# A decoder layer in split fp32 on one core: LN1's high parts written from PSUM, first weights cast behind h, Silu's table loaded early

## The chip, the cores and the metric

The kernel runs on one core of a Trainium2 chip. The metric is the device time of one execution in microseconds. A core has TensorE (PE, with PEld its weight loads), VectorE (DVE), ScalarE (ACT), GpSimd (POOL) and SyncE (SP), which issues most of the DMAs. Every engine works through its own list of instructions in order and waits on semaphores for the others.

## What is computed

One layer of a decoder with 512 prompt positions and 8 decode rows, model width 1024, all in fp32:

```python
h = x * (1 + scale) + shift                      # adaLN, from silu(c) @ w_ada + b_ada
aq, ak, av, mq, mk, mv, mo, mi, mf = split(h @ w_in)
att = block_sparse_attention(aq, ak, av)         # decode rows read a paged K/V cache
mem = mlstm(mq, mk, mv, mi, mf)                  # 4 heads of 128, matrix memory C, state n, m
mix = concat(att, norm(mem) * g * sigmoid(mo)) @ w_out
x = layernorm(ALPHA * x + (1 + g1) * mix)        # LN1
h = x * (1 + sc2) + sh2                          # called h2 below
f = (silu(h @ w_gate) * (h @ w_up)) @ w_down     # FFN, inner width 2816
y = layernorm(ALPHA * x + (1 + g2) * f)
```

Returned are y, the new K/V rows and the new mLSTM states, for prompt and decode rows.

## The kernel before

**Products.** An fp32 product is made of three passes (`three`, L400): each operand is split into a high part, rounded to the matmul type fp32r, and a low part, the rest, and high x high, high x low and low x high are added in PSUM. The high part is a cast on ScalarE, the low part a subtraction on VectorE. For weights this is `prepare_one` (cast whi at L232, subtraction wlo at L233, tiles of 128x1024), for activations `split_hidden` (L403: cast at L404, subtraction at L405).

**Order.** The program's order is made when it is built. Pieces of work are generators ("lanes"); each `tick` lets every lane that is due run to its next `yield n`, which puts it off by n ticks, then prepares one weight tile and issues the weight loads for which a buffer is free, all on SP's queue in one fixed stream. Between the ticks TensorE's large products are written. So the number behind `yield` decides behind which pieces of the products a lane's next instructions stand, on every engine.

**First phase** (`first_phase`). The first input projection runs over five chunks of the 1024 input columns while adaLN's first two vectors are still being made. For chunk i: `first_ada` (product with w_ada, copy of ada_sb on ScalarE, transposes ps_adat on TensorE), the split of the chunk's weights (`first_split`: whi, wlo of wq at L534 and L535, the same for wk_s at L537), then `first_h`: adaT, two operations of VectorE from ps_adat (L494); h on VectorE and, at the same time, its high part straight from x on ScalarE (L511); its low part; the decode rows' h (hsT) and its small cast hT_hi at the end (L520, L404). `first_main` are the products of six column blocks; those with 0 to 3 use whi and wlo.

**Decode rows of the mLSTM** (`sample_mlstm`). It ends with h8, which four small transposes (L1543, ps_h) bring into the layout of the output product's operand. Around them on TensorE stand the passes of the output product's first half, and the last prompt states: products ps_C (L1197) that ScalarE copies to Csb (L1200), and the sums ps_n (L1168), whose four rows are copied by ScalarE and VectorE in turn (L1172). When the decode rows are there, `ln_rows` may load the rows lg and lb of LN1's affine part, which ScalarE multiplies later (L1620).

**LN1** (`ln1_tile`, one per tile of 128 positions). The output product has two halves (`out_product`): tiles 0 and 1, then tiles 2 and 3. When both column halves of a tile are out of PSUM and added to x (`residual`, L1631 and L1632), `ln1_tile` makes the statistics and normalises x, and some ticks later, for each half of 512 columns: four transposes into one PSUM bank (L1699, ps_h), four operations of ScalarE with scale a2 and bias b2 that write v in SBUF (L1703), the two casts h_hi (L404) and the two subtractions h_lo (L405). These are h2's parts for the FFN.

**FFN.** `ffn_first` begins while tiles 2 and 3 are in LN1; its Silu (L1813) loads ScalarE's table for that function when it comes to it. From there on TensorE runs through the FFN's weights.

Of the kernel before, what the change touches and what calls it, by code (L numbers as in the profile page):

```python
# [13 lines left out]
AF = mybir.ActivationFunctionType  # L14
ALU = mybir.AluOpType
AX = mybir.AxisListType.X

P = 128
# [28 lines left out]
def decoder_layer(  # L47
# [61 lines left out]
    TT = nc.vector.tensor_tensor  # L109
    TS = nc.vector.tensor_scalar  # L110
# [3 lines left out]
    ACT = nc.scalar.activation  # L114
# [288 lines left out]
    def split_hidden(dst_hi, dst_lo, v):  # L403
        ACOPY(out=dst_hi, in_=v)  # L404
        TT(out=dst_lo, in0=v, in1=dst_hi, op=ALU.subtract)  # L405
# [151 lines left out]
    def first_phase():  # L557
        n = len(chunks)
        for i in range(n):
            sb = first_ada(i)  # L560
            if i:
                first_split(i)
            if i + 3 < n:
                load_first(i + 3)
                if i + 4 == n:
                    later_loads()
            elif i + 2 >= n:
                pump_loads()
            if i:
                first_main(i - 1, (3,))  # L570
            first_h(i, sb)
            if i:
                first_main(i - 1, (4, 5))
            if i + 1 == n:
                prepare_one()
                prepare_one()
            first_main(i, (0, 1, 2))
        first_main(n - 1, (3, 4, 5))
# [817 lines left out]
    junk = cst.tile([P, P], F32, name="junk")  # L1396
# [99 lines left out]
    def sample_mlstm(lag):  # L1496
# [16 lines left out]
        ps = yield from lane_bank("ps_nu")  # L1513
# [23 lines left out]
                bias=s[:, 13, h:h + 1])  # L1537
        yield 1
        TT(out=h8, in0=h8, in1=o_s, op=ALU.mult)
        yield 2  # L1540
        ps = yield from lane_bank("ps_h8")
        for h in range(HM):
            nc.tensor.transpose(ps[:, ts(h, 8)], h8[:, ts(h, P)], ident[:NB, :NB])  # L1543
# [35 lines left out]
    a2 = cst.tile([P, KD, 9], F32, name="a2")  # L1579
# [107 lines left out]
    def ln1_tile(t):  # L1687
        s = ln1_stats[t]
        nc.vector.bn_stats(out=s[:, 6:12], in_=x1[t][:, 512:D])
        nc.vector.bn_aggr(out=s[:, 12:14], in_=s[:, 0:12])  # L1690
        rsqrt(s[:, 14:15], s[:, 13:14])
        TS(out=x1[t], in0=x1[t], scalar1=s[:, 12:13], scalar2=s[:, 14:15], op0=ALU.subtract, op1=ALU.mult)
        yield 9 if t < 2 else 5
        while not h2_hi:
            yield 1
        for half in range(2):
            ps = yield from lane_bank("ps_h2")
            for kk in range(4):
                nc.tensor.transpose(ps[:, ts(kk, P)], x1[t][:, ts(4 * half + kk, P)], ident)  # L1699
            v = yield from slot(rows, "v2", spare=1)  # L1700
            for kk in range(4):
                k = 4 * half + kk
                ACT(out=v[:, ts(kk, P)], in_=ps[:, ts(kk, P)], func=AF.Identity,  # L1703
                    scale=a2[:, k, 8:9], bias=b2[:, k, 8:9])
            banks.put(ps)
            v3 = v[:, 0:512].rearrange("p (k q) -> p k q", q=P)
            for i in range(2):
                split_hidden(h2_hi[2 * half + i][:, :, ts(t, P)], h2_lo[2 * half + i][:, :, ts(t, P)],
                             v3[:, 2 * i:2 * i + 2, :])
            rows.put(v)  # L1710
        h2_done[0] += 1
        while not ffn.get(("f", 1)):
            yield 1
        yield 2 * t
        for n in range(2):
            PT_(out=x1[t][:, ts(n, 512)], in0=x1[t][:, ts(n, 512)], in1=big2["lg"][n], op=ALU.mult)
            PT_(out=x1[t][:, ts(n, 512)], in0=x1[t][:, ts(n, 512)], in1=big2["lb"][n], op=ALU.add)
        x1_done[0] += 1
# [393 lines left out]
    nc.gpsimd.memset(ffn["fsT"], 0.0)  # L2112
    ffn["sacc"] = get("sacc", [512])
    state["spill"] = 2
    ffn_first(2)
    state["spill"] = 0

# [81 lines left out]
```

## Time and profile before

| | us |
|---|---|
| median of 3 runs | 788.52 (786.09 to 791.42) |
| the profiled execution's own time | 786.77 |
| its span in the profile | 785.1 |
| mean granted clock of TensorE | 0.993 of full |
| TensorE busy | 752.9 (96%) |
| VectorE busy | 405.3 (52%) |
| ScalarE busy | 276.5 (35%) |

All rows come from the one profiled execution, and their times count from the start of its span. What lies between span and execution time is 1.7 us.

A row of a timeline gives the start, the duration, engine, line, operation, result<-operands and how many instructions are drawn together; the brackets at the end give the time that the engine stood idle before it and what ended that. Line numbers are those of the kernel before; in the changed kernel they are one or two smaller or some larger, as the diff moves them.

### The profile page before, as it was taken

What the parts mean: (1) busy time and instruction counts of PE and PEld (TensorE: products, weight loads), DVE (VectorE), ACT (ScalarE), POOL (GpSimd) and SP (SyncE); (2) the same over time, 40 slices, a digit from 0 to 9 for tenths busy, and PEclk for the clock granted to TensorE, in tenths of its full rate; (3) what the DMA queues carried; (4) which work ended last, traced back from release to release, by engine and by line L of the source; (5) the groups of instructions that cost most, each with busy time, mean ns of one, the idle gap of its engine ahead of it and who ended that gap; (6) DMA issues with size and microseconds to landing.
All of it is one profiled execution on the core that took longest, in us unless ns stands there. A gap on an engine that the chain in (4) does not pass through costs nothing.

```text
span 785.1 us, 14709 instructions
## 1 busy us (share of the span) xinstructions
PE 752.9 (96%) x5798; PEld 620.7 (79%) x5798; DVE 405.3 (52%) x850; ACT 276.5 (35%) x560; POOL 140.3 (18%) x163
## 2 busy tenths in 40 slices
PE   8899999899989998899899999999999999999995
PEld 6678667688755667656799977999987799999675
DVE  3442378977345487588653434333332342332687
ACT  2341466545343346536442211223221122322300
POOL 2010235342000122000029413100001130000011
PEclk9999999999999999999999999999999999999998
DMA  8965885664678968746523425323223323223002
GB/s 334 375 221 146 264 266 176 213 215 136 196 244 282 292 236 172 274 152 192 148 59 105 136 84 154 87 84 106 91 74 89 97 81 108 82 81 108 1 30 81
DMA packets 105906, 123.11 MB, mean 157 GB/s; under 512 B 8220, under 2 KB 65696, under 8 KB 105836
## 3 DMA queue, kind: packets, MB, share of 16 engines
q1 hardware_dynamic: 97796, 112.97, 45.9%
q10 hardware_dynamic: 7976, 9.20, 3.4%
q8 instruction: 45, 0.74, 0.4%
q14 instruction: 25, 0.20, 0.1%
q0 software_dynamic: 64, 0.01, 0.0%
HBM read 114.98 MB, written 7.17 MB: 156 GB/s over the span
## 4 chain that ended last, share of the span: by engine, by line
PE 70%; DVE 10%; DMA 4%; ACT 4%; issue 3%; SPq 1%; POOL 1%; ACTq 0%; POOLq 0%; DVEq 0%
PE acc L657 35%; PE acc L398 21%; DVE wlo L233 2%; PE ps_dn L420 1%; PE ps_ada L412 1%; PE accl L398 1%; DVE rtmp L1631 1%; PE ps_sc L815 1%; ACT whi L232 1%; DVE x L1632 1%; PE ps_pt L848 1%; PE ps_o L878 1%; DMA raw<-in_w_ada_dram 1%; PE ps_num L1084 1%; DMA s_scr<-s_sb 1%
## 5 line engine op out<-in xcount | busy, mean ns | idle before, releaser
L233 DVE TENSOR_TENSOR wlo<-raw,whi 128x1024 fp32r<-128x1024 f32 x104 | 137.0, 1324 | 120.8 <-ACT whi L232 114.0
L232 ACT CAST whi<-raw 128x1024 fp32r<-128x1024 f32 x104 | 107.9, 1049 | 156.4 <-issue 65.7
L657 PE MATMUL acc<-h_lo,whi 128*128 128x256 f32 (+1 forms) x640 | 129.0, 283 | 0.0
L657 PE MATMUL acc<-h_hi,wlo 128*128 128x256 f32 (+1 forms) x640 | 129.0, 283 | 0.0
L657 PE MATMUL acc<-h_hi,whi 128*128 128x256 f32 (+1 forms) x640 | 128.7, 282 | 0.0
L657 PEld LDWEIGHTS acc<-h_hi,whi 128*128 128x128 f32 x640 | 99.1, 188 | 2.7 <-issue 2.5
L657 PEld LDWEIGHTS acc<-h_hi,wlo 128*128 128x128 f32 x640 | 99.5, 188 | 0.0
L657 PEld LDWEIGHTS acc<-h_lo,whi 128*128 128x128 f32 x640 | 98.6, 188 | 0.0
L1236 POOL TENSOR_TENSOR kpage<-kpage,qb 128x512 f32<-128x512 f32 x32 | 43.3, 1374 | 74.9 <-DMA kpage<-in_cache_k_dram 72.0
L1780 DVE TENSOR_TENSOR vf<-acc,vf 128x256 f32<-128x256 f32 x20 | 8.5, 425 | 73.6 <-PE acc L657 73.6
L398 PE MATMUL acc<-whi,f_hi 128*128 128x512 f32 x112 | 45.3, 405 | 0.0
L398 PE MATMUL acc<-wlo,f_hi 128*128 128x512 f32 x112 | 44.3, 395 | 0.0
L398 PE MATMUL acc<-whi,f_lo 128*128 128x512 f32 x112 | 44.2, 394 | 0.0
L398 PE MATMUL acc<-whi,hT_hi 128*128 128x512 f32 x96 | 43.1, 449 | 0.0
L1786 POOL COPY fsT<-vf 128x8 f32<-128x8 f32 x20 | 4.8, 240 | 193.4 <-DVE vf L1781 193.4
L404 ACT CAST f_hi<-vf 128x512 fp32r<-128x512 f32 (+1 forms) x24 | 14.0, 585 | 68.0 <-DVE vf L1781 62.0
L398 PE MATMUL acc<-whi,hT_lo 128*128 128x512 f32 x96 | 38.0, 396 | 0.0
L398 PE MATMUL acc<-wlo,hT_hi 128*128 128x512 f32 x96 | 37.8, 394 | 0.0
L1632 POOL TENSOR_TENSOR x<-x,rtmp 128x512 f32<-128x512 f32 x16 | 26.0, 1646 | 65.1 <-DVE rtmp L1631 64.7
L657 PE MATMUL acc<-hT_hi,whi 128*128 128x256 f32 (+1 forms) x160 | 35.7, 304 | 0.0
L657 PE MATMUL acc<-hT_lo,whi 128*128 128x256 f32 (+1 forms) x160 | 32.3, 283 | 0.0
L657 PE MATMUL acc<-hT_hi,wlo 128*128 128x256 f32 (+1 forms) x160 | 32.3, 283 | 0.0
(403 smaller groups left out, 1407.0 us busy)
## 6 DMA issues: line engine op xcount, KB each, us to landing
raw<-in_w_ada_dram SPq DMA_DIRECT2D x32, 512.0 KB
raw<-in_w_in_dram SPq DMA_DIRECT2D x22, 512.0 KB
raw<-in_w_gate_dram SPq DMA_DIRECT2D x44, 256.0 KB
raw<-in_w_up_dram SPq DMA_DIRECT2D x44, 256.0 KB
raw<-in_w_down_dram SPq DMA_DIRECT2D x22, 512.0 KB
raw_a<-in_ada_first_dram SPq DMA_DIRECT2D x16, 512.0 KB
kpage<-in_cache_k_dram SPq DMA_DIRECT2D x32, 256.0 KB
vpage<-in_cache_v_dram SPq DMA_DIRECT2D x32, 256.0 KB
```

The source lines that it names most:

```text
L232: ACOPY(out=t.hi_t, in_=t.raw)
L233: TT(out=t.lo_t, in0=t.raw, in1=t.hi_t, op=ALU.subtract)
L398: mm(ps, lhsT=a, rhs=b, start=start and i == 0, stop=stop and i == n - 1)
L404: ACOPY(out=dst_hi, in_=v)
L412: mm(ps[32 * c:32 * c + 32, 0:P], lhsT=lhs[:, k0 + kk, :], rhs=raw3[:, kk, ts(c, P)], start=start and kk == 0, stop=stop and kk == nk - 1, ...
L420: mm(ps[32 * c:32 * c + 32, 0:256], lhsT=lhs[:, k0 + kk, :], rhs=raw3[:, kk, ts(n, 256)], start=start, stop=stop, tile_position=(0, 32 * c))
L657: mm(accs[d, hf][:, 0:hi - lo], lhsT=w, rhs=two(xx, k)[:, lo:hi], start=k == 0 and i == 0, stop=k == 7 and i == 2)
L815: mm(bs[e][:, 0:n], lhsT=two(qT, pair)[eh, ts(qt, P)], rhs=two(kT, pair)[eh, 0:n], start=True, stop=True, tile_position=(64 * e, 0))
L848: nc.tensor.transpose(ps[:, ts(kt, P)], pr[:, ts(kt, P)], ident)
L1236: PT_(out=ks[i - 4], in0=ks[i - 4], in1=qb, op=ALU.mult)
L1632: (PT_ if pool_add else TT)(out=dst, in0=dst, in1=tmp, op=ALU.add)
L1780: TT(out=v[:, 0:HALF], in0=a[:, 0:HALF], in1=v[:, 0:HALF], op=ALU.mult)
```

## The change

Four edits. (1) In the first phase, from the second chunk on, `first_split` comes after `first_h`. (2) In `sample_mlstm` the lane waits four ticks, not two, ahead of its transposes. (3) In `ln1_tile` ScalarE writes the high part directly from PSUM, in four operations; VectorE computes v from the same PSUM bank, and the low part is v less the high part. The two casts from v are gone. (4) Ahead of the FFN's first products ScalarE runs a Silu on one element of a scratch tile.

```diff
--- before.py
+++ after.py
@@ -558,8 +558,6 @@
         n = len(chunks)
         for i in range(n):
             sb = first_ada(i)
-            if i:
-                first_split(i)
             if i + 3 < n:
                 load_first(i + 3)
                 if i + 4 == n:
@@ -570,6 +568,7 @@
                 first_main(i - 1, (3,))
             first_h(i, sb)
             if i:
+                first_split(i)
                 first_main(i - 1, (4, 5))
             if i + 1 == n:
                 prepare_one()
@@ -1537,7 +1536,7 @@
                 bias=s[:, 13, h:h + 1])
         yield 1
         TT(out=h8, in0=h8, in1=o_s, op=ALU.mult)
-        yield 2
+        yield 4
         ps = yield from lane_bank("ps_h8")
         for h in range(HM):
             nc.tensor.transpose(ps[:, ts(h, 8)], h8[:, ts(h, P)], ident[:NB, :NB])
@@ -1700,13 +1699,15 @@
             v = yield from slot(rows, "v2", spare=1)
             for kk in range(4):
                 k = 4 * half + kk
-                ACT(out=v[:, ts(kk, P)], in_=ps[:, ts(kk, P)], func=AF.Identity,
+                ACT(out=h2_hi[k // 2][:, k % 2, ts(t, P)], in_=ps[:, ts(kk, P)], func=AF.Identity,
                     scale=a2[:, k, 8:9], bias=b2[:, k, 8:9])
+                TS(out=v[:, ts(kk, P)], in0=ps[:, ts(kk, P)], scalar1=a2[:, k, 8:9], scalar2=b2[:, k, 8:9],
+                   op0=ALU.mult, op1=ALU.add)
             banks.put(ps)
             v3 = v[:, 0:512].rearrange("p (k q) -> p k q", q=P)
             for i in range(2):
-                split_hidden(h2_hi[2 * half + i][:, :, ts(t, P)], h2_lo[2 * half + i][:, :, ts(t, P)],
-                             v3[:, 2 * i:2 * i + 2, :])
+                hi, lo = h2_hi[2 * half + i][:, :, ts(t, P)], h2_lo[2 * half + i][:, :, ts(t, P)]
+                TT(out=lo, in0=v3[:, 2 * i:2 * i + 2, :], in1=hi, op=ALU.subtract)
             rows.put(v)
         h2_done[0] += 1
         while not ffn.get(("f", 1)):
@@ -2112,6 +2113,8 @@
     nc.gpsimd.memset(ffn["fsT"], 0.0)
     ffn["sacc"] = get("sacc", [512])
     state["spill"] = 2
+
+    ACT(out=junk[0:1, 0:1], in_=junk[0:1, 0:1], func=AF.Silu)
     ffn_first(2)
     state["spill"] = 0
```

Since lanes set the order, edit (2) moves more than it touches. The places on which the steps stand follow; a row is an engine's instruction (source line, operation, result<-operands, size, what it waits for), in the order of the list, and "x3" stands for three like rows.

ScalarE in the first phase, third chunk, before: ada_sb is the copy of the chunk's adaLN product, whi and wk_s are its weights, the two ACTIVATEs are the high part of h.

```order
L470 COPY ada_sb<-ps_ada 128x128 [waits PE_49]
L534 CAST whi<-wq 128x1024 [waits DMAHW0_49]
L537 CAST wk_s<-wk_90 128x512 [waits DMAHW1_49,Activation_49]
L511 ACTIVATE hT_hi<-xT,adaT 128x512 [waits DMAHW7_49,DVE_49]
L511 ACTIVATE hT_hi<-xT,adaT 128x512
L404 CAST hT_hi<-hsT 128x2x8 [waits DVE_49]
```

ScalarE there, with the change:

```order
L470 COPY ada_sb<-ps_ada 128x128 [waits PE_49]
L511 ACTIVATE hT_hi<-xT,adaT 128x512 [waits DMAHW7_49,DVE_49,Activation_49]
L511 ACTIVATE hT_hi<-xT,adaT 128x512
L404 CAST hT_hi<-hsT 128x2x8 [waits DVE_49]
L534 CAST whi<-wq 128x1024 [waits DMAHW0_49]
L537 CAST wk_s<-wk_90 128x512 [waits DMAHW4_49,DMAHW1_49]
```

The weights' casts have moved behind the decode rows' cast from hsT, which waits for VectorE. VectorE's wlo and the low part of wk_s have moved likewise, behind hsT.

TensorE before, around the decode rows' transposes (ps_h_4335; `acc` are passes of the output product):

```order
L398 MATMUL acc<-whi,mixM_hi 128x512
L398 MATMUL acc<-wlo,mixM_hi 128x512
L398 MATMUL acc<-whi,mixM_lo 128x512
L1543 MATMUL ps_h_4335<-ident,h_4172 128x8 [waits DVE_49,Activation_49]
L1543 MATMUL ps_h_4335<-ident,h_4172 128x8 [waits Activation_49] x3
L1197 MATMUL ps_C<-mk,mv_3173 128x128 [waits Activation_49]
L1197 MATMUL ps_C<-mk,mv_3173 128x128
L1197 MATMUL ps_C<-mk,mv_3174 128x128 x2
L1132 MATMUL ps_hm<-ident,hm 128x128 [waits Activation_49]
L1132 MATMUL ps_hm<-ident,hm 128x128 x3
L398 MATMUL acc<-whi,mixM_hi 128x512
```

TensorE from the same point with the change (h_4172 is the same tile):

```order
L398 MATMUL acc<-whi,mixM_hi 128x512
L398 MATMUL acc<-wlo,mixM_hi 128x512
L398 MATMUL acc<-whi,mixM_lo 128x512
L1196 MATMUL ps_C<-mk,mv_3173 128x128 [waits Activation_49]
L1196 MATMUL ps_C<-mk,mv_3173 128x128
L1196 MATMUL ps_C<-mk,mv_3174 128x128 x2
L1131 MATMUL ps_hm<-ident,hm 128x128 [waits Activation_49]
L1131 MATMUL ps_hm<-ident,hm 128x128 x3
L398 MATMUL acc<-whi,mixM_hi 128x512
```

and some rows further down:

```order
L1196 MATMUL ps_C<-mk,mv_3173 128x128 [waits Activation_49]
L1196 MATMUL ps_C<-mk,mv_3173 128x128
L1196 MATMUL ps_C<-mk,mv_3174 128x128 x2
L1542 MATMUL ps_h_4394<-ident,h_4172 128x8 [waits DVE_49]
L1542 MATMUL ps_h_4394<-ident,h_4172 128x8 x3
L398 MATMUL acc<-whi,mixM_hi 128x512
L398 MATMUL acc<-wlo,mixM_hi 128x512
```

The four transposes have moved behind the next ps_C, ps_hm, six passes, ps_n and one more ps_C. On SP's queue the loads of lg and lb have moved with them, behind the loads of a w_ada tile, of xs and of the two Gs tiles; on ScalarE the products of lg and lb, which stood ahead of a whi cast before LN1's first tile, stand behind the h_hi of tiles 0 and 1, as the second of the next two fences shows.

ScalarE in LN1 before, tile 1 and what follows it (h_hi_4576 to 4579 are the four quarters of h2's high part):

```order
L1703 ACTIVATE v_4690<-ps_h_4685,b_229,a_228 128x128 [waits PE_49]
L1703 ACTIVATE v_4690<-ps_h_4685,b_229,a_228 128x128 x3
L404 CAST h_hi_4576<-v_4690 128x2x128 [waits Activation_49]
L404 CAST h_hi_4577<-v_4690 128x2x128 [waits Activation_49]
L1703 ACTIVATE v_4704<-ps_h_4699,b_229,a_228 128x128 [waits DVE_49,PE_49]
L1703 ACTIVATE v_4704<-ps_h_4699,b_229,a_228 128x128 x3
L404 CAST h_hi_4578<-v_4704 128x2x128 [waits Activation_49]
L404 CAST h_hi_4579<-v_4704 128x2x128 [waits Activation_49]
L232 CAST whi<-raw 128x1024 [waits DMAHW7_49]
L232 CAST whi<-raw 128x1024 [waits DMAHW0_49,PE_49]
```

ScalarE there with the change:

```order
L1702 ACTIVATE h_hi_4576<-ps_h_4685,b_229,a_228 128x128 [waits PE_49]
L1702 ACTIVATE h_hi_4576<-ps_h_4685,b_229,a_228 128x128 [waits DVE_49]
L1702 ACTIVATE h_hi_4577<-ps_h_4685,b_229,a_228 128x128 [waits DVE_49] x2
L1702 ACTIVATE h_hi_4578<-ps_h_4701,b_229,a_228 128x128 [waits PE_49]
L1702 ACTIVATE h_hi_4578<-ps_h_4701,b_229,a_228 128x128 [waits DVE_49]
L1702 ACTIVATE h_hi_4579<-ps_h_4701,b_229,a_228 128x128 [waits DVE_49] x2
L1619 ACTIVATE lg<-lg 128x512
L1619 ACTIVATE lg<-lg 128x512 [waits DMAHW0_49]
L1619 ACTIVATE lb<-lb 128x512 [waits DMAHW7_49]
L1619 ACTIVATE lb<-lb 128x512 [waits DMAHW1_49]
L232 CAST whi<-raw 128x1024 [waits DMAHW7_49,Activation_49]
L232 CAST whi<-raw 128x1024 [waits DMAHW0_49,PE_49,Activation_49]
```

The casts are gone, and each of a bank's later three operations now waits for VectorE. VectorE there with the change (before, these are four L405 rows and the wlo rows):

```order
L1704 TENSOR_SCALAR v_4690<-ps_h_4685,a_228,b_229 128x128 [waits Activation_49] x4
L1710 TENSOR_TENSOR h_lo_4580<-v_4690,h_hi_4576 128x2x128 [waits DVE_49]
L1710 TENSOR_TENSOR h_lo_4581<-v_4690,h_hi_4577 128x2x128 [waits DVE_49]
L1704 TENSOR_SCALAR v_4706<-ps_h_4701,a_228,b_229 128x128 [waits Activation_49] x4
L1710 TENSOR_TENSOR h_lo_4582<-v_4706,h_hi_4578 128x2x128 [waits DVE_49]
L1710 TENSOR_TENSOR h_lo_4583<-v_4706,h_hi_4579 128x2x128 [waits DVE_49]
L233 TENSOR_TENSOR wlo<-raw,whi 128x1024 [waits DMAHW7_49,Activation_49]
L233 TENSOR_TENSOR wlo<-raw,whi 128x1024 [waits DMAHW0_49,Activation_49]
L233 TENSOR_TENSOR wlo<-raw,whi 128x1024 [waits DMAHW2_49,DMAHW1_49,Activation_49]
```

Each of the four L1704 operations of a bank waits for ScalarE. Their values show which instruction each waits for: VectorE's operation on a block of 128 columns waits for ScalarE's on that block, and ScalarE's on the next block for VectorE's on this one; both read one PSUM bank. The wlo of the next weights stands behind all sixteen.

Silu's table: the added Silu stands on ScalarE behind the decode rows' casts (L404, from vs) and ahead of the two casts of whi that preceded the FFN's first Silu before.

## Rows read from the trace of the kernel before

**Rows 1.** The page, part 1: busy time, share and instructions of each engine

```profile
PE 752.9 (96%) x5798; PEld 620.7 (79%) x5798; DVE 405.3 (52%) x850; ACT 276.5 (35%) x560; POOL 140.3 (18%) x163
```

**Rows 2.** The timeline ahead of the decode rows' transposes, all engines

```profile
321.11 0.25 ACT L1200 COPY Csb<-ps_C 128x128 f32<-128x128 f32 x1
323.19 0.38 PE L1543 MATMUL ps_h<-ident,h 8*128 8x8 f32 x4 [2.45 <-DVE h L1539]
```

**Rows 3.** The timeline of ScalarE, 350 to 387 us

```profile
350.21 1.14 ACT L1620 ACTIVATE lg<-lg 128x512 f32<-128x512 f32 x2
...
356.07 1.50 ACT L1703 ACTIVATE v<-ps_h,b,a 128x128 f32<-128x128 f32 x4 [1.95 <-PE ps_h L1699]
357.46 0.72 ACT L404 CAST h_hi<-v 128x256 fp32r<-128x256 f32 x2
...
364.01 2.09 ACT L232 CAST whi<-raw 128x1024 fp32r<-128x1024 f32 x2
...
385.18 1.28 ACT L1813 ACT_TABLE_LOAD   x1
386.48 0.38 ACT L1813 ACTIVATE vf<-acc 128x256 f32<-128x256 f32 x1
```

**Rows 4.** The timeline of VectorE, 359 to 396 us

```profile
359.25 1.43 DVE L405 TENSOR_TENSOR h_lo<-v,h_hi 128x256 fp32r<-128x256 f32 x4
360.59 0.69 DVE L1631 TENSOR_TENSOR rtmp<-acc,G 128x512 f32<-128x512 f32 x1
...
365.18 2.36 DVE L233 TENSOR_TENSOR wlo<-raw,whi 128x1024 fp32r<-128x1024 f32 x2 [0.49 <-ACT whi L232]
...
384.25 2.36 DVE L233 TENSOR_TENSOR wlo<-raw,whi 128x1024 fp32r<-128x1024 f32 x2 [0.78 <-ACT whi L232]
...
395.27 0.76 DVE L405 TENSOR_TENSOR h_lo<-v,h_hi 128x256 fp32r<-128x256 f32 x2 [1.25 <-ACT h_hi L404]
```

**Rows 5.** The timeline of TensorE at the FFN's head

```profile
395.75 0.39 PE L398 MATMUL acc<-h_lo,whi 128*128 128x264 f32 x1
```

**Rows 6.** The timeline of the first phase, fourth chunk, all engines

```profile
35.66 1.23 DVE L535 TENSOR_TENSOR wlo<-wq,whi 128x1024 fp32r<-128x1024 f32 x1 [7.60 <-ACT whi L534]
35.73 0.27 PE L487 MATMUL ps_adat<-ident,ada_sb 128*128 128x128 f32 x1
...
37.41 0.25 DVE L494 SCALAR_TENSOR_TENSOR adaT<-ps_adat,cols 128x18 f32<-128x18 f32 x2
...
39.69 0.39 PE L398 MATMUL acc<-hT_hi,wlo 128*128 128x512 f32 x1
...
40.27 0.20 ACT L404 CAST hT_hi<-hsT 128x16 fp32r<-128x16 f32 x1 [1.05 <-DVE hsT L520]
```

**Rows 7.** The timeline of the first phase, third chunk, ScalarE

```profile
21.96 1.05 ACT L534 CAST whi<-wq 128x1024 fp32r<-128x1024 f32 x1 [0.32 <-DMA wq<-in_w_in_dram]
```

**Rows 8.** Windows: stretch, length, busy PE PEld DVE ACT POOL, PEclk, DMA share, GB/s

```profile
324.00:326.00 2.00, 2.00 (x12) 2.00 (x11) 1.33 (x2) 0.70 (x2) 0.00 (x0) 0.50 0.90 302
322.00:328.00 6.00, 4.81 (x22) 4.27 (x22) 3.67 (x6) 2.88 (x5) 0.00 (x0) 0.72 0.74 236
```

**Rows 9.** The timeline of the copies of ps_n, ScalarE and VectorE

```profile
329.18 0.25 ACT L1172 COPY nsb<-ps_n 1x128 f32<-1x128 f32 x1 [2.14 <-PE ps_n L1168]
329.47 0.28 DVE L1172 COPY nsb<-ps_n 1x128 f32<-1x128 f32 x1 [1.71 <-ACT nsb L1172]
329.79 0.26 ACT L1172 COPY nsb<-ps_n 1x128 f32<-1x128 f32 x1 [0.35 <-DVE nsb L1172]
```

**Rows 10.** Line L1703: count, ns min/median/max, first and last start

```profile
L1703 ACT ACTIVATE v<-ps_h,b,a x32: 447/477/537, 356.1 to 394.5; 128x128 f32<-128x128 f32 x32
```

**Rows 11.** VectorE's groups by form: busy us, mean ns of one, idle before

```profile
L1422 DVE SCALAR_TENSOR_TENSOR C<-kq,gvs,C 128x128 f32<-128x128 f32 x32 | 9.5, 356 | 0.0
L1426 DVE SCALAR_TENSOR_TENSOR junk<-kq,C 128x128 f32<-128x128 f32 x32 | 9.4, 294 | 0.8
...
L1021 DVE TENSOR_SCALAR mkT<-acc 128x256 f32<-128x256 f32 x4 | 1.7, 417 | 0.9 <-PE acc L657 0.9
```

## The prediction

> **What bounds the kernel now.** I read the page's busy shares first: TensorE is busy for 96% of the span [rows 1], so the change counts only where TensorE waits, or where something that it will wait for becomes later. Then I followed the chain of waits and the timelines through the three places that the diff touches. In the first phase TensorE waits for h of each chunk. Before the output product's end it stands still for 2.45 us ahead of four small transposes that wait for VectorE [rows 2]. Between 356 and 396 us, where LN1's tiles are turned into h2, the reader is to see that ScalarE and VectorE are nearly full and that the chain runs through them: ScalarE makes four half tiles without a gap from 356.07 to 364.01, 1.99 us each [rows 3], VectorE's wlo of the next weight tiles follow at 365.18, and the FFN's head goes on only at 395.75, when the first h_lo of the last half tile is there [rows 4, 5]. From there on TensorE does not wait in any way that matters, so a delay at 395.75 is a delay of the end.
>
> The sum is made against the profiled execution, 786.8 us; the median of the three runs, 788.5, lies 1.7 above it.
>
> **First phase.** Casting the weights behind h lets adaT follow the transposes at once. In the fourth chunk the transposes end at 36.00, and adaT began only at 37.41, since wlo and the cast of wk stood ahead of it [rows 6]. But the weights are now last, and not merely behind h: the order on ScalarE puts the cast of whi behind the small cast of hT_hi from hsT, which waits for all of VectorE's work on h. From adaT's start to that cast's end the rows have 40.27 + 0.20 - 37.41 = 3.06 us [rows 6]. Then come whi, 1.05 [rows 7], wlo, 1.23 [rows 6], and some 0.03 at each of three hand-overs. The chunk's first product with wlo, at 39.69 before, starts at 36.00 + 3.06 + 1.05 + 1.23 + 0.09 = 41.43: 1.74 us later. The fifth chunk repeats the pattern. The second has half the columns, and in the third the cast of wq waited 0.32 us for its DMA anyway [rows 7]; I put 0.7 on the two together. The next chunk's transposes stand behind these products on TensorE, so the delays add: **+4.2**. Ends: 0, if waits for DMA in the attention stages take it up, and 4.2 + 2 x 1.7 = 7.6, if the clock falls in two of the longer stalls (1.7 from the next paragraph).
>
> **The transposes of the decode rows.** With `yield 4` they stand behind two more state products, the sums ps_n and the passes between. TensorE, free at 323.19 - 2.45 = 320.74, then meets a product that waits for a copy of ScalarE which ends at 321.36 [rows 2]: with the hand-over some 0.65 us instead of 2.45, so -1.8. After the long stall the granted clock was 0.50 for all of 324 to 326 us, the lower of its two levels, 1.2 GHz, and 0.72 in the mean of 322 to 328 [rows 8]: about 6.00 x 0.28 = 1.7 us lost. If that goes too the gain is 3.5. VectorE, which is dense from 331 us on, will not follow all of it: **-2.5**, ends -3.5 and 0. The loads of lg and lb go behind four other DMAs on the same queue; nothing needs them before 350 us.
>
> **LN1, the large term.** Each half tile loses two casts (0.72 us together on ScalarE [rows 3]) and gains four operations of VectorE that read the same PSUM bank as ScalarE's four. The waits in the order are what matters: VectorE's operation for a block waits for ScalarE's of that block, and ScalarE's for the next block waits for VectorE's of this one. Two streams that could each run at their own pace become one chain of eight steps with a hand-over after each. The trace of before has one such chain, the copies of ps_n: ScalarE ends at 329.43 and VectorE starts at 329.47, VectorE ends at 329.75 and ScalarE starts at 329.79 [rows 9]. So a hand-over is 0.04 us.
>
> The price of a pair: ScalarE's operation, with nothing to overlap with, 0.45 (the least of the 32 [rows 10]). For VectorE's there is no row. The nearest are a TENSOR_SCALAR from PSUM of twice the columns, 0.417, and two operations of 128 columns in SBUF that differ in one scalar taken from memory, 0.294 without and 0.356 with it [rows 11]. The new one has half the columns of the first and two such scalars: about 0.28 + 2 x 0.06 = 0.40. The pair is then 0.45 + 0.04 + 0.40 + 0.04 = **0.93**. Ends: 0.61, the whole pair of the copies [rows 9], and 0.54 + 0.08 + 0.43 = 1.05 with the longest of ScalarE's 32 and a VectorE operation as long as that of twice the columns.
>
> A half tile on VectorE is three pairs, the fourth operation, and the two h_lo (0.76 [rows 4]), less 0.09 by which the next operation starts before the last has ended (359.25 + 1.43 against 360.59): 2.79 + 0.40 + 0.76 - 0.09 = **3.85**, against 1.99 on ScalarE before.
>
> Tiles 0 and 1. The first new operation stands where h_lo stood, at 359.25. Four half tiles and the three residual operations between them (three of 0.69; one row stands for them [rows 4]) end at 359.25 + 15.4 + 2.07 = 376.7. ScalarE's last is 0.76 + 0.40 + 0.04 earlier, 375.5. Behind it stand lg's and lb's four products now, which used to run in ScalarE's free time at 350: the first two take 1.14 and the second two the same [rows 3], 2.2 with their overlap. Then the cast of whi, 1.05. wlo starts at 378.8, not at 365.18 [rows 4]: +13.6. TensorE needs it for the second half of the output product and has nothing else queued ahead, so VectorE's chain behind it (residual, statistics, the decode rows) shifts whole.
>
> Tiles 2 and 3. Silu's table is loaded now ahead of the two casts of whi; before, it came behind them, at 385.18 [rows 3]. Both places are on the chain, since ScalarE is free only until the decode rows' h arrives and the load stands behind that: 1.28 and a tiny Silu of 0.2 put wlo 1.5 later and give the 1.28 back only to ScalarE, which is then not the one waited for. wlo starts at 384.25 + 13.6 + 1.5 = 399.35, the first new operation 2.3 later at 401.65; three half tiles, three pairs, the fourth operation and the first of two h_lo (0.42) are 11.55 + 2.79 + 0.40 + 0.42 = 15.2, and 0.15 goes to the copy of ada_sb between the tiles. TensorE goes on at 417.0, not at 395.75 [rows 5]: **+21.2**. With the pair at 0.61 the same steps give +12.9, at 1.05 +24.4.
>
> On the table load rows and skill differ. In the row the Silu starts 0.02 us behind the load's end, so I count 1.28 [rows 3]. The Trainium skill (ScalarE: Activation LUTs, section on what ACT_TABLE_LOAD costs) adds a drain of about 1380 ns to 1283 ns of load; by that the sum would be 1.4 us higher. The trace does not show the drain, so it is not in the sum.
>
> **Clock.** TensorE will stand still for 10 us or more in LN1, where before it stood 1.6 and 2.0. After 2.45 us it fell to the lower level [rows 8]; once such a fall, as long as that one, on the chain: **+1.7**, ends 0 and 3.4.
>
> Sum: 786.8 + 4.2 - 2.5 + 21.2 + 1.7 = **811.4**.
>
> **Rivals.** (a) The reads run side by side, the waits being met early. ScalarE then needs 1.39 us per half tile (356.07 to 357.46 [rows 3]), and VectorE only its own work: 16 operations of 0.34 behind each other push wlo from 365.18 to 369.6, and the end of LN1 comes out 4.6 later. 786.8 + 4.2 - 2.5 + 4.6 = 793, not slower by 1%. It decides from a half tile of about 2 us. For it: the first phase makes h on both engines from one SBUF tile without such waits. Against it: every one of the new operations carries a wait for the other engine, and the copies of ps_n kept to it. Chance 0.08. The Trainium skill (Advanced Engine Details and Errata, section on bank collisions) says that both engines can read PSUM at full bandwidth if no bank collides; here both read one bank, so that rule promises nothing.
> (b) LN1's first two tiles are covered by the output product that TensorE has queued, and only tiles 2 and 3 pay: 21.2 - 13.6 = 7.6, so 786.8 + 4.2 - 2.5 + 7.6 = 796. Against it: wlo of that product's own weights stands behind the new operations. Chance 0.12.
> (c) The upper prices with two falls of the clock in LN1 and a first phase that loses more: 786.8 + 5.0 + 24.4 + 3.4 = 819.6. Chance 0.13.
> My forecast, 803 to 817, has 0.65; 0.02 is left for a gain that I see no way to.
>
> **The numbers.** 811 is the likeliest case. The range 799 to 819 leaves out (a), (b) and the far part of (c). A measurement of this kernel can tell about 1% from no change, 8 us. Slower by more: the forecast, (c), and half of (b): 0.84. Within 1%: (a), the other half of (b): 0.13. Faster 0.03.
>
> **What the changed profile would show.** h_hi from PSUM and v on VectorE alternate without overlap, some 0.9 us from one h_hi to the next; whi's cast behind the products of lg and lb, and wlo some 13 us later than at 365; TensorE idle for about 10 us in the output product's second half; the FFN's head 20 us later. In the first phase the product with wlo starts 5.5 us after the transposes, where it was 3.7. No stall ahead of the decode rows' transposes. If h_hi and v overlap, or a half tile takes 2 us, the large term is wrong; if the pair stands at 0.6 or 1.05, its price.

## The result, and the profile after

The changed kernel takes 812.74 us (median of four executions, 811.23 to 817.91) against 789.97 us for the kernel before, run beside it: a ratio of 1.033, with a 95% interval of 1.029 to 1.036. The ratio, 25.8 us, is what the sums below use; the quotient of the two medians alone is 1.029, 22.8 us, at the lower end of the interval. The forecast was 811, with 799 to 819 as its range. Two executions far from all others, one of d_table (825.77 us) and one of a2_lg20 (2743.79 us), are in no ratio below.

The profiled execution of the change is the longest of the four: 817.91 us, a span of 816.2. The other three have spans near 810 and 812. So its 31.1 us over the profiled execution of before are more than the change costs on the median, and each stage below is compared with that in mind.

The page, part 1, of the changed kernel, answers to [rows 1]:

```profile
PE 763.8 (94%) x5798; PEld 627.2 (77%) x5798; DVE 418.9 (51%) x882; ACT 274.3 (34%) x545; POOL 139.3 (17%) x163
```

TensorE has the same 5798 matmuls and is busy for 10.9 us longer: they ran at a lower clock in places. VectorE has 32 instructions more, ScalarE 15 fewer. The other 20.2 of the 31.1 us are time in which TensorE stands still.

LN1, first. The timeline of the changed kernel, ScalarE and VectorE in the first half tile, answers to the half tiles of [rows 3, 4]:

```profile
366.28 0.40 DVE L1704 TENSOR_SCALAR v<-ps_h,a,b 128x128 f32<-128x128 f32 x1
366.72 0.46 ACT L1702 ACTIVATE h_hi<-ps_h,b,a 128x128 fp32r<-128x128 f32 x1 [3.15 <-DVE v L1704]
367.21 0.41 DVE L1704 TENSOR_SCALAR v<-ps_h,a,b 128x128 f32<-128x128 f32 x1 [0.53 <-ACT h_hi L1702]
367.65 0.46 ACT L1702 ACTIVATE h_hi<-ps_h,b,a 128x128 fp32r<-128x128 f32 x1 [0.48 <-DVE v L1704]
368.15 0.41 DVE L1704 TENSOR_SCALAR v<-ps_h,a,b 128x128 f32<-128x128 f32 x1 [0.53 <-ACT h_hi L1702]
...
369.41 0.75 DVE L1710 TENSOR_TENSOR h_lo<-v,h_hi 128x256 fp32r<-128x256 f32 x2
...
370.08 0.40 DVE L1704 TENSOR_SCALAR v<-ps_h,a,b 128x128 f32<-128x128 f32 x1
```

Read the brackets: each engine stands idle for about as long as the other works, 0.53 and 0.48 us, and each names the other. From one h_hi to the next it is 367.65 - 366.72 = 0.93 us, and from half tile to half tile 370.08 - 366.28 = 3.80, where it was 1.99.

What that does to TensorE, in the timeline of the changed kernel after the last of tiles 0 and 1:

```profile
382.40 1.14 ACT L1619 ACTIVATE lg<-lg 128x512 f32<-128x512 f32 x2
...
383.44 1.14 ACT L1619 ACTIVATE lb<-lb 128x512 f32<-128x512 f32 x2
384.48 1.98 ACT L232 CAST whi<-raw 128x1024 fp32r<-128x1024 f32 x2
385.54 2.36 DVE L233 TENSOR_TENSOR wlo<-raw,whi 128x1024 fp32r<-128x1024 f32 x2 [1.93 <-ACT whi L232]
...
385.56 0.79 PE L398 MATMUL acc<-whi,mixM_hi 128*128 128x512 f32 x1 [10.80 <-ACT whi L232]
```

TensorE stands still for 10.80 us until the next weights' cast, which stood behind sixteen alternating pairs and the four products of lg and lb. In tiles 2 and 3 the table load is on the way as well, and the FFN's head, at 395.75 in [rows 5], comes at 425.25 (the timelines of ScalarE, VectorE and TensorE):

```profile
404.92 0.52 ACT L404 CAST h_hi<-vs 128x16 fp32r<-128x16 f32 x4 [10.79 <-DVE vs L1754]
405.46 1.28 ACT L2117 ACT_TABLE_LOAD   x1
406.76 0.20 ACT L2117 ACTIVATE junk<-junk 1x1 f32<-1x1 f32 x1
406.87 1.98 ACT L232 CAST whi<-raw 128x1024 fp32r<-128x1024 f32 x2
```

```profile
407.93 2.36 DVE L233 TENSOR_TENSOR wlo<-raw,whi 128x1024 fp32r<-128x1024 f32 x2 [2.27 <-ACT whi L232]
```

```profile
421.46 0.59 PE L398 MATMUL acc<-h_lo,whi 128*128 128x264 f32 x1 [3.20 <-DVE h_lo L1710]
...
425.25 0.59 PE L398 MATMUL acc<-h_lo,whi 128*128 128x264 f32 x1 [0.79 <-DVE h_lo L1710]
```

The granted clock behind the two stalls, in windows of the changed kernel (columns as in [rows 8]). The values are means between the lower level, 0.50, and the full clock; before, all of 360 to 406 us was at 1.00:

```profile
386.00:396.00 10.00, 9.53 (x43) 5.58 (x43) 7.06 (x11) 2.72 (x4) 0.53 (x1) 0.71 0.55 160
...
421.00:433.00 12.00, 10.75 (x60) 10.45 (x61) 7.65 (x17) 5.05 (x10) 0.19 (x1) 0.65 0.28 77
```

In the first phase, fourth chunk, the timeline of TensorE answers to [rows 6]: the product with wlo comes 43.88 - 38.18 = 5.70 us after the transposes' end (37.91 + 0.27), where it was 3.69.

```profile
37.91 0.27 PE L487 MATMUL ps_adat<-ident,ada_sb 128*128 128x128 f32 x1
...
42.62 0.50 PE L398 MATMUL acc<-hT_hi,whi 128*128 128x512 f32 x1 [1.67 <-ACT whi L534]
...
43.88 0.79 PE L398 MATMUL acc<-hT_hi,wlo 128*128 128x512 f32 x1 [0.52 <-DVE wlo L535]
```

### The profile page after: what moved, and what is told of

It reads as the page before. It is cut to its first block, busy times and chain, and to the rows that moved or that the text cites. A ratio compares the mean times of both kernels' runs of the same rounds, so it can differ in the third digit from the quotient of the medians.

```text
span 816.2 us, 14722 instructions
## 1 busy us (share of the span) xinstructions
PE 763.8 (94%) x5798; PEld 627.2 (77%) x5798; DVE 418.9 (51%) x882; ACT 274.3 (34%) x545; POOL 139.3 (17%) x163
## 4 chain that ended last, share of the span: by engine, by line
PE 43%; DVE 5%; issue 2%; ACT 1%; POOL 1%; DMA 0%; POOLq 0%; ACTq 0%; DVEq 0%
PE acc L656 28%; PE acc L398 12%; PE ps_dn L420 1%; PE accl L398 1%; DVE v L1704 1%; DVE rtmp L1630 1%; ACT h_hi L1702 1%; DVE wlo L233 1%; DVE x L1631 1%; POOL ls L1161 1%; DMA raw<-in_w_gate_dram 0%; DVE x L1886 0%; DVE h_lo L1710 0%; DVE ls L1877 0%; DVE xs L1631 0%
## 5 line engine op out<-in xcount | busy, mean ns | idle before, releaser
L656 PE MATMUL acc<-h_hi,whi 128*128 128x256 f32 (+1 forms) x640 | 128.9, 283 | 0.0
L656 PE MATMUL acc<-h_hi,wlo 128*128 128x256 f32 (+1 forms) x640 | 128.8, 283 | 0.0
L656 PE MATMUL acc<-h_lo,whi 128*128 128x256 f32 (+1 forms) x640 | 128.8, 283 | 0.0
L656 PEld LDWEIGHTS acc<-h_hi,whi 128*128 128x128 f32 x640 | 99.2, 188 | 2.7 <-issue 2.5
L656 PEld LDWEIGHTS acc<-h_lo,whi 128*128 128x128 f32 x640 | 99.1, 188 | 0.0
L656 PEld LDWEIGHTS acc<-h_hi,wlo 128*128 128x128 f32 x640 | 99.0, 189 | 0.0
L404 ACT CAST f_hi<-vf 128x512 fp32r<-128x512 f32 (+1 forms) x24 | 14.0, 585 | 69.9 <-DVE vf L1782 62.4
L656 PE MATMUL acc<-hT_hi,whi 128*128 128x256 f32 (+1 forms) x160 | 36.2, 308 | 0.0
L656 PE MATMUL acc<-hT_hi,wlo 128*128 128x256 f32 (+1 forms) x160 | 32.7, 287 | 0.0
L656 PE MATMUL acc<-hT_lo,whi 128*128 128x256 f32 (+1 forms) x160 | 32.6, 286 | 0.0
```

The costliest lines, as they stand in the source:

```text
L656: mm(accs[d, hf][:, 0:hi - lo], lhsT=w, rhs=two(xx, k)[:, lo:hi], start=k == 0 and i == 0, stop=k == 7 and i == 2)
```

## The experiments

Ratios are against the kernel before, on the same chip in the same hour, with a 95% interval. Microseconds are the ratio's times 788, the median of before in these hours.

**The four parts alone.** Each kernel is the kernel before with one of the change's edits.

```diff
# a_first, in first_phase
             sb = first_ada(i)
-            if i:
-                first_split(i)
...
             first_h(i, sb)
             if i:
+                first_split(i)
                 first_main(i - 1, (4, 5))
# b_yield, in sample_mlstm
-        yield 2
+        yield 4
# d_table, ahead of the FFN
+    ACT(out=junk[0:1, 0:1], in_=junk[0:1, 0:1], func=AF.Silu)
     ffn_first(2)
# c_ln1: the hunk of ln1_tile, as in the change
```

The first phase: 

> Only the first phase's part of the change (weights of the chunks split behind h). Theory: the products with wlo start 1.7 to 2.0 us later in each of the three late chunks, and the clock falls once more; the trace of the whole change shows the first phase's end 7.6 us later, so this part alone costs +4 to +8 us against before. Rival: the attention stages behind it wait for DMA in any case and take the delay up, 0 to +1 us.

Measured: 1.0080 (1.0052 to 1.0108), +6.3 us. The theory holds, and the rival is excluded. The timeline of TensorE shows the late product with wlo, 43.13 - 37.76 = 5.37 us after the transposes of the fourth chunk (5.42 in the third and the fifth), and the next transposes:

```profile
37.49 0.27 PE L487 MATMUL ps_adat<-ident,ada_sb 128*128 128x128 f32 x1
...
43.13 0.59 PE L398 MATMUL acc<-hT_hi,wlo 128*128 128x512 f32 x1 [0.52 <-DVE wlo L535]
...
51.99 0.27 PE L487 MATMUL ps_adat<-ident,ada_sb 128*128 128x128 f32 x1
```

The windows show the clock:

```profile
24.00:50.00 26.00, 20.85 (x174) 15.37 (x176) 9.31 (x20) 6.27 (x11) 1.50 (x1) 0.87 0.95 341
...
43.00:48.00 5.00, 4.87 (x14) 3.88 (x15) 0.68 (x2) 0.00 (x0) 0.00 (x0) 0.66 1.05 373
```

The same of the kernel before, a window of its clock and the next transposes on TensorE:

```profile
24.00:50.00 26.00, 23.48 (x203) 18.01 (x203) 11.58 (x29) 8.05 (x14) 1.50 (x1) 0.93 0.96 344
```

```profile
46.90 0.27 PE L487 MATMUL ps_adat<-ident,ada_sb 128*128 128x128 f32 x1
```

Before, all of 40 to 50 us was at 1.00. From the fourth chunk's product with wlo to the next transposes it was 46.90 - 39.69 = 7.21 us ([rows 6]), and it is 51.99 - 43.13 = 8.86 here: that is 1.65 us beside the late wlo itself, and the stretch at 0.66 accounts for it (5 x 0.34 = 1.7).

The transposes: 

> Only the decode rows' transposes later (yield 4). Theory: the stall of 2.45 us ahead of them and the low clock behind it go, -2.5 to -3.8 us against before. Rival: VectorE is dense behind that place and starts LN1 when it did, 0 +- 0.5 us.

Measured: 0.9981 (0.9958 to 1.0003), -1.5 us. The interval, -3.3 to +0.2, takes in no change as well as the smaller numbers of the theory; the time alone does not decide. The stall has shrunk to 0.57 us, and LN1 starts 4.6 us earlier in the profile, 1.2 of them from the first phase, so the rival, that VectorE starts LN1 when it did, does not hold. But the timeline of ScalarE shows where about half of it goes back:

```profile
358.85 0.79 ACT L404 CAST h_hi<-v 128x256 fp32r<-128x256 f32 x2
359.45 1.23 ACT L1620 ACTIVATE lg<-lg 128x512 f32<-128x512 f32 x2
360.51 1.22 ACT L1620 ACTIVATE lb<-lb 128x512 f32<-128x512 f32 x2
361.55 2.06 ACT L232 CAST whi<-raw 128x1024 fp32r<-128x1024 f32 x2
```

The products of lg and lb stand between the last high part and the weights' cast for which VectorE and TensorE wait: 2.1 us.

LN1: 

> Only LN1's part (high part from PSUM on ScalarE, v from the same bank on VectorE). Theory: the chain of hand-overs, 0.94 us for a pair, is the large term also without the others: 21.2 + 1.7 us, less 2.2 for the products of lg and lb, which stay ahead of LN1 here, and less 1.5 for Silu's table, so about +19 us against before (+16 to +22). Rival: most of the loss in LN1 came from what the other parts put behind ScalarE's high parts (lg, lb, the table), and this alone costs +5 to +10 us.

Measured: 1.0260 (1.0234 to 1.0286), +20.5 us. The theory holds; the rival is excluded.

The table: 

> Only Silu's table loaded ahead of the FFN's first products. Theory: both places are on the chain, and with ScalarE as the bound in LN1's tiles 2 and 3 only the added Silu of 0.2 us counts, 0 to +1.5 us against before. Rival: the load finds ScalarE idle and the 1.28 us come back, -1.3 us.

Measured: 1.0001 (0.9979 to 1.0022). That fits the theory, but the rival's -1.3 lies inside the interval of -1.7 to +1.7 too, so the profile decides. In the timeline of ScalarE the load starts 1.4 us ahead of the casts of whi instead of behind them, and what follows the casts starts where it did (386.49 against 386.48 in [rows 3]); the 1.28 us do not come back:

```profile
383.20 1.28 ACT L2116 ACT_TABLE_LOAD   x1
384.50 0.20 ACT L2116 ACTIVATE junk<-junk 1x1 f32<-1x1 f32 x1
384.61 1.97 ACT L232 CAST whi<-raw 128x1024 fp32r<-128x1024 f32 x2
386.49 0.37 ACT L1813 ACTIVATE vf<-acc 128x256 f32<-128x256 f32 x1
```

The parts add, within the noise of some 2 us in each: 6.3 - 1.5 + 20.5 + 0.1 = 25.4 us; the whole change measured 0.0327 x 788 = 25.8.

**Is it the alternation, or VectorE's work?** Two kernels with LN1's part alone, and the same sixteen operations more on VectorE per pair of tiles. The lines are shown against c_ln1, with arguments cut to "...".

```diff
# c3_order: the same bank, written as two loops
             for kk in range(4):
                 k = 4 * half + kk
                 ACT(out=h2_hi[k // 2][:, k % 2, ts(t, P)], in_=ps[:, ts(kk, P)], ...)
+            for kk in range(4):
+                k = 4 * half + kk
                 TS(out=v[:, ts(kk, P)], in0=ps[:, ts(kk, P)], ...)
# c2_banks: one loop, the transposes written to two banks
-            ps = yield from lane_bank("ps_h2")
+            ps, ps2 = yield from lane_bank("ps_h2", 2)
+            for dst in (ps, ps2): ...                      # four transposes into each
...
-                TS(out=v[:, ts(kk, P)], in0=ps[:, ts(kk, P)], ...)
+                TS(out=v[:, ts(kk, P)], in0=ps2[:, ts(kk, P)], ...)
```

> LN1's part alone, same instructions on the same bank, but written as ScalarE's four and then VectorE's four, so that a bank is handed over once and not seven times. Theory: the alternation is what costs; ScalarE then runs ahead at 1.4 us per half tile, VectorE needs three times 0.34, once 0.41 and 0.67 for the two low parts = 2.1 us instead of 0.67, and the FFN's head comes 3.5 to 5 us later than before, not 21: +3.5 to +5 us. Rival: VectorE's sixteen operations from PSUM cost as much in any order, +15 us or more.

Measured: 1.0063 (1.0040 to 1.0086), +5.0 us. The order alone is worth 0.0197 x 788 = 15.5 of the 20.5 us. In the timeline, ScalarE and VectorE of this kernel:

```profile
359.93 5.94 ACT L1703 ACTIVATE h_hi<-ps_h,b,a 128x128 fp32r<-128x128 f32 x16 [1.95 <-PE ps_h L1699]
...
363.09 1.36 DVE L1707 TENSOR_SCALAR v<-ps_h,a,b 128x128 f32<-128x128 f32 x4
364.37 0.75 DVE L1713 TENSOR_TENSOR h_lo<-v,h_hi 128x256 fp32r<-128x256 f32 x2
365.04 1.36 DVE L1707 TENSOR_SCALAR v<-ps_h,a,b 128x128 f32<-128x128 f32 x4
365.72 2.28 ACT L232 CAST whi<-raw 128x1024 fp32r<-128x1024 f32 x2
```

The theory holds, at its upper end, and the rival is excluded. ScalarE makes all sixteen without a gap in 5.94 us, and the weights' cast follows at once; a half tile on VectorE takes 365.04 - 363.09 = 1.95, its own work and nothing else. The 5 us that are left are VectorE's: it comes to the weights' wlo at 372.92 in this trace, 6 us after the first of the two casts.

> LN1's part alone in the alternating order, but with the transposes written to two banks, one for ScalarE's reads and one for VectorE's (16 x 4 small products of TensorE more than needed otherwise, counted as 32 more in all). Theory: no bank is shared, so no operation waits for the other engine's read, and it ends like the one-hand-over version, +3.5 to +6 us against before. Rival: the two streams of reads slow each other or the order of the operations costs as such, +15 us or more.

Measured: 1.0061 (1.0034 to 1.0087), +4.8 us. In the alternating order too the loss goes when no bank is shared: in its timeline VectorE starts while ScalarE is still reading (from 359.29 to 362.19), with 1.36 us for its four as in the last kernel.

```profile
359.29 2.90 ACT L1704 ACTIVATE h_hi<-ps_h,b,a 128x128 fp32r<-128x128 f32 x8 [1.01 <-PE ps_h L1700]
...
360.49 1.36 DVE L1706 TENSOR_SCALAR v<-ps_h,a,b 128x128 f32<-128x128 f32 x4
```

The theory holds here too. So it is neither VectorE's work nor the alternation as such, but one bank handed to and fro.

**The whole change with the order alone altered** (the two loops above in the changed kernel). 

> The whole change, with only LN1's eight operations per bank written as ScalarE's four and then VectorE's four. Theory: the parts add as measured alone: +6.2 (first phase), -1.5 (transposes), 0 (table) and +4.9 (LN1 with one hand-over) = +9.6 us against before, so 13 to 16 us of the change's 25 are the alternation. Rival: in the whole change the products of lg and lb and the table load stand on LN1's path too and the order buys less, +15 us or more.

Measured: 1.0087 (1.0058 to 1.0117), +6.9 us. The parts add to 6.3 - 1.5 + 5.0 + 0.1 = 9.9; with the noise of each part the two agree. Against the change's 1.0327 the order is worth 0.0240 x 788 = 18.9 us. That is above the theory's 13 to 16, though with the two intervals it may be as little as 15. The profiles say the same: from LN1's first operation to the FFN's first L656 product it is 437.28 - 363.11 = 74.2 us in the change and 414.31 - 358.95 = 55.4 here. The rival is wrong, as the timelines of ScalarE and VectorE show:

```profile
366.83 2.02 ACT L232 CAST whi<-raw 128x1024 fp32r<-128x1024 f32 x2
```

```profile
371.96 3.48 DVE L233 TENSOR_TENSOR wlo<-raw,whi 128x1024 fp32r<-128x1024 f32 x3
```

The products of lg and lb, from 364.74 us, are over and the weights' cast behind them has begun at 366.83, while VectorE is busy with its half tiles up to 371.96. So these products cost nothing here, and in the change, where the cast waits for them, they cost 384.48 - 382.40 = 2.1 us: that is part of what the order is worth there.

**Where in the chunk the first weights are split.**

```diff
# a_hs: in first_h, the split ahead of hsT for every chunk
         put(xT, hT)
-        if i == 0:
-            first_split(0, 1)
+        first_split(i, 1 if i == 0 else None)
         TT(out=hsT[:, ks, 0:8], ...)
# a2: in first_h, split in the middle of h, for every chunk as for the first
-        if i == 0:
-            first_split(0, 0)
+        first_split(i, 0)                                # wq, ahead of h's high part
...
         put(xT, hT)
-        if i == 0:
-            first_split(0, 1)
+        first_split(i, 1)                                # wk, ahead of hsT
# both, in first_phase
             sb = first_ada(i)
-            if i:
-                first_split(i)
```

> First phase alone, with the weights' split behind h's high and low part but ahead of the decode rows' h (hsT) and its cast. Theory: the 3.06 us up to the cast from hsT are what holds whi back; here whi starts when h's high part is done, some 2.3 us behind adaT, wlo is ready some 0.8 us earlier per chunk than with the change, and of the +6.2 us measured for that part +2.5 to +4.5 are left. Rival: the place within h does not matter, since VectorE has the same work ahead of the products anyway; +6 us as before.

Measured: 0.9999 (0.9979 to 1.0019): nothing is left of the 6.3 us. The direction was right and the size too small. The timeline of TensorE has the product with wlo 37.88 - 33.77 = 4.11 us after the transposes, 1.26 earlier than with the part of the change, not 0.8, and the windows show that the clock does not fall:

```profile
33.50 0.27 PE L487 MATMUL ps_adat<-ident,ada_sb 128*128 128x128 f32 x1
...
37.88 0.50 PE L398 MATMUL acc<-hT_hi,wlo 128*128 128x512 f32 x1 [0.54 <-DVE wlo L534]
```

```profile
24.00:50.00 26.00, 23.27 (x206) 17.18 (x207) 11.95 (x25) 8.32 (x14) 2.46 (x2) 1.00 0.94 341
```

The profiled execution of before had 0.93 there. So wlo still comes 4.11 - 3.69 = 0.42 us later than before in this chunk, and against that execution a clock that stays up gives 26 x 0.07 = 1.8 us back: that nothing is left is the sum of such delays and such gains.

> First phase alone, with each chunk's weights split in the middle of h, as the kernel has it for its first chunk: the cast of whi ahead of h's high part (ScalarE is waiting then), wlo between h and its low part on VectorE. Theory: adaT follows the transposes as in the change, and wlo is no longer the last; both low parts are ready 3.4 to 4.1 us behind the transposes, as before (3.4 and 3.7), so -1 to +1 us. Rival: every step between adaT and the low part of h costs the chunk its full time, wlo's 1.23 us each: +3 to +5 us.

Measured: 0.9981 (0.9955 to 1.0008), -1.5 us: just beyond the theory's -1 to +1, and no more than noise by itself. The rival, +3 to +5, is excluded.

**Towards a faster kernel.**

```diff
# b_lg20: with yield 4 ahead of the decode rows' transposes, in ln_rows
-            yield 12
+            yield 20
             for r_ in g_ + b_:
                 nc.scalar.mul(out=r_, in_=r_, mul=scale)
# b_lg20_mix: also, in ln1_tile, the two loops of c3_order where t >= 2 and half == 0, the old form elsewhere
# a2_lg20: b_lg20 with the first phase of a2
```

> The decode rows' transposes later, and the products of lg and lb put off by 20 ticks instead of 12, which brings them behind four weight casts into ScalarE's idle 11 us. In the trace with the later transposes alone these products stood between the high parts and the weights' cast and took 2.1 us of the 4.6 gained. Theory: they come back, 3.5 to 5 us faster than before. Rival: the gain is lost elsewhere (decode rows, DMA), and it stays at -1.5 us.

Measured: 0.9965 (0.9937 to 0.9993), -2.8 us: faster, and less than the theory's 3.5 to 5, which the interval (-5.0 to -0.6) reaches. In the profile the 2.0 us between LN1's start and the FFN's first L657 product are back (402.0 - 352.1 = 49.9 against 403.4 - 351.5 = 51.9 without it); in the timeline of ScalarE, lg now fills an idle stretch:

```profile
359.45 0.79 ACT L404 CAST h_hi<-v 128x256 fp32r<-128x256 f32 x2
360.06 2.08 ACT L232 CAST whi<-raw 128x1024 fp32r<-128x1024 f32 x2
...
367.56 1.15 ACT L1620 ACTIVATE lg<-lg 128x512 f32<-128x512 f32 x2
```

> The same, and in tiles 2 and 3 the first half tile of each takes its high part from PSUM (four of ScalarE, then four of VectorE), the second half as before: ScalarE is the bound there, with VectorE idle for more than half. Theory: ScalarE saves 0.6 us in two half tiles, up to 1.2 us at the FFN's head; 4.5 to 6 us faster than before. Rival: VectorE's low part of the mixed halves comes later than ScalarE's saving, no gain over the run beside it.

Measured: 0.9962 (0.9939 to 0.9984), -3.0 us, the same as its neighbour and short of the 4.5 to 6 forecast. The rival holds: TensorE's wait at the FFN's head, 2.10 us for ScalarE's h_hi without the mix, is now 2.40 for VectorE's h_lo.

```profile
389.48 0.39 PE L398 MATMUL acc<-h_lo,whi 128*128 128x264 f32 x1 [2.40 <-DVE h_lo L1717]
```

> The same first phase together with the later transposes and the later products of lg and lb (that pair alone: -0.35%). Theory: the parts add, as those of the change did; 2 to 4 us faster than before. Rival: what the first phase gains or loses is taken up by the attention stages behind it, and it stands where the pair alone stands.

Measured: 0.9929 (0.9904 to 0.9954), -5.6 us, the fastest of all and faster than both kernels; more than the 2 to 4 us forecast, of which the interval (-7.6 to -3.6) takes in the upper end. The gains add within the noise: the parts gave -1.5 and -2.8, and the sum of 4.3 lies in the interval. The rival, that the kernel stands where b_lg20 stands, fits worse: -2.8 lies outside this interval, though the two intervals overlap.

## Why the prediction was right

**The mechanism of LN1** was right as told, and its price too. The pair was put at 0.93 us and is 0.93 to 0.94; a half tile at 3.85 and is 3.80. VectorE's new operation, for which there was no row, takes 0.41 (0.40 forecast from the rows nearest to it), ScalarE's 0.46 (0.45), and a hand-over 0.03 to 0.04 (0.04): ScalarE's 367.65 + 0.46 is 368.11 and VectorE starts at 368.15. The rival (a), reads side by side, is what c2_banks makes of it with two banks, and there it comes out near its forecast of +4.6. That the alternation on one bank is the cause, and not VectorE's added work, is shown by c3_order and c2_banks.

On the waits the Trainium skill (PSUM — Partial Sum Buffer, section on bank collisions) says that two engines must not be on one bank, in the same partitions, at once, reads against reads included, and that a program should guard PSUM by bank. The traces agree in what a program does about it: with one bank no operation of the one engine overlaps the other's on it, with two they run together. What the chip does where nothing guards a bank, no run here shows.

**Tiles 0 and 1, then 2 and 3.** LN1's first operation of ScalarE came 7.0 us later than before (363.11 against 356.07). From there the terms are, forecast and measured: the first late wlo, +13.6 and 385.54 - 365.18 - 7.0 = +13.3; the table load, +1.5 and 2.27 - 0.78 = +1.5 of VectorE's idle time ahead of the second wlo; the half tiles up to the FFN's head, 21.2 - 13.6 - 1.5 = +6.1 and (425.25 - 407.93) - (395.75 - 384.25) = +5.8. The rival (b), that only the second pair pays, is refuted by the 10.80 us for which TensorE stood still.

**The clock** was the mis-sized term of LN1. The size of a fall was right, their number was not: one fall was taken, 1.7 us; two came. In the stretch at 0.71 the way to the second wlo grew by 407.93 - 384.25 - 20.4 - 1.5 = 1.8 us more (20.4 is the delay of the first wlo, 385.54 - 365.18). Between the FFN's head and its steady stretch, at 0.65, 1.9 were lost: the first L656 product of the change starts at 437.3, L657 of before at 405.9, which is 31.4 us later, and the head was 425.25 - 395.75 = 29.5 later. The two rows are from the views of the tile acc, with first and last start:

```profile
L656 PE MATMUL acc<-h_hi,whi x640: 274/282/393, 437.3 to 757.1; 128*128 128x256 f32 x160
```

```profile
L657 PE MATMUL acc<-h_hi,whi x640: 275/282/388, 405.9 to 725.9; 128*128 128x256 f32 x160
```

Together 3.7, where the upper end given was 3.4.

**The first phase** was put at +4.2, with 7.6 as the end if the clock falls too; alone it measures +6.3, with an interval of 4.1 to 8.5. The steps to the late wlo were right: 5.43 us from the transposes, and 5.37 and 5.70 in the two traces. The clock's share belonged into the sum and not into its upper end: in a_first the fall behind the fourth chunk alone cost the 1.65 us shown there, and the end had 1.7 for one. That the weights were last, and not merely behind h, is shown by a_hs, which moves them ahead of hsT, has the product with wlo 1.26 us earlier and, with the clock that it keeps up, loses nothing.

**The transposes** were put at -2.5 and measure -1.5 alone, with an interval that takes in both. The prediction said that the products of lg and lb would stand behind ScalarE's high parts and counted their 2.2 us in LN1; in the part alone they cost the same there. In b_lg20, where they stand in an idle stretch, the later transposes measure -2.8, near the term. In the trace of the change no wait is left ahead of the transposes, and the clock is 1.00 from 316 to 336 us, where it was 0.91.

**The table load.** The sum took the row's 1.28 and no drain. In the traces of before, of the change, of d_table and of b_lg20, ScalarE's next operation starts 0.02 us after the load's end (405.46 + 1.28 = 406.74, Silu at 406.76), and the load starts no more than 0.02 us after the operation ahead of it. The drain of the Trainium skill (ScalarE: Activation LUTs, section on what ACT_TABLE_LOAD costs) is in none of them. That the place does not matter where ScalarE is the bound, d_table shows; that it costs 1.5 where VectorE is, only the trace of the change tells, and no run took it out alone.

**The sum.** A rise of 811.4 - 786.8 = 24.6 us was forecast; the ratio gives 25.8, the medians 22.8, the profiled executions 31.1. The mechanism is right, but that 811.4 lies 1.3 from 812.74 is in part luck: the first phase and the clock in LN1 were each about 2 us too small, the steps of LN1 together 0.6 too large, and the sum started from 786.8, while the kernel before measured 789.97 beside the change. Of rival (c) the two falls of the clock and the larger first phase came and the upper prices did not; its 819.6 takes nothing for the transposes. The chances of a change within 1% add to 0.08 + 0.06 = 0.14, not to the 0.13 given.

One thing stays open: from the end of the first phase to LN1's first operation the profiled execution of the change took 363.11 - 66.31 = 296.8 us, where five others with the later transposes took 292.3 to 294.2. Those 3 us are not explained. Eight kernels with the early transposes, that of before among them, took 297.2 to 301.1 in the same stretch, so one execution differs from another by as much, and three executions of the changed kernel were 4 to 7 us shorter; they need not belong to the change.

## What to carry to other kernels

When two engines are to read one PSUM bank, look at the waits in the order before counting operations: written in turn, block by block, the two streams become one chain, and moving one loop (all of one engine's reads, then all of the other's) took 15.5 of its 20.5 us away without changing an instruction. A step that "frees" an engine is worth nothing where the work goes to the engine that stands next on the same path: in the best order LN1's part still cost 5 us, since VectorE got 1.3 us more per half tile and ScalarE 0.5 less. And put the clock into the sum wherever a stall on TensorE grows: three falls of 1.65 to 1.9 us each are read off above, and the prediction's sum had one.

## What the runs showed of the hardware

- Four of VectorE's operations from PSUM (128x128, scale and offset from memory) take 1.36 us one behind the other, so one starts 0.32 us after the last; alone each takes 0.41. In a chain with hand-overs the 0.41 counts, without them the 0.32.
- ScalarE writes the rounded high part straight from PSUM in the time of the plain one: sixteen in 5.94 us, four in 1.50 in [rows 3].
- Stalls of like length went with different clocks. In a_hs TensorE stood still for 1.49 and then 0.53 us in the third chunk, and the granted clock was 1.00 from 24 to 50 us. In a_first it stood still for 1.33 and then 0.52 us in the fourth chunk, and the clock was 0.66 from 43 to 48 us. So the length of a stall alone does not tell here whether the clock falls.
